# Four weight sums of an S5 layer moved from GpSimd to accumulating transfers, and one unit's state products put ahead of its Toeplitz products

## The chip, the cores and the metric

The kernel runs on one core of one Trainium2 chip, as one launch. The metric is the device time of a whole execution in microseconds; the median of several runs is compared. Times inside an execution are those of one profiled execution, counted from its first instruction.

The engines are named as in the profile: PE is TensorE's matmul and PEld its weight load, DVE is VectorE, ACT ScalarE, POOL GpSimd, SP SyncE, which only issues transfers. A queue with a q behind its name (ACTq, SPq) is an engine's issuing of transfers.

## The reference

One layer of a diffusion backbone over 1024 latent tokens of width 1024 and a prefix of 256 context tokens: a bidirectional S5 mixer (a diagonal complex state-space model in 64 groups of 16 channels with 64 states each), then a SwiGLU network, each behind an RMS norm with shift, scale and gate.

```python
lam_bar = jnp.exp(lam * jnp.exp(log_step)[:, None])
b_bar = ((lam_bar - 1.0) / lam)[..., None] * lax.complex(b_re, b_im)
bu = jnp.einsum('lgh,gnh->lgn', u, b_bar)
h = associative_scan(...)                      # h[l] = lam_bar * h[l-1] + bu[l]
y = jnp.einsum('lgn,ghn->lgh', h, c_mat).real  # forward and backward summed
...
y = y + d_skip * h
g = gelu(y);  y = g * sigmoid(g @ w_glu + b_glu)
x = x + gate * y
x = x + gate2 * ((silu(h2 @ w1) * (h2 @ w3)) @ w2)
```

## The kernel before

The sequence is cut into chunks of T = 8 tokens: 32 chunks of context, 128 of latent tokens. States are computed only at chunk ends. What a chunk adds within itself is a Toeplitz matrix per group; what the state at its start adds is a product with output weights. So the mixer's output for one group is a sum of two products: inputs of the chunk times a Toeplitz matrix (line 936), and states times output weights (line 926).

The 64 groups form four quarters q (16 groups each) and eight units k (8 groups each, two units to a quarter). Two lists of short words, `PROG1` and `PROG2`, are read from left to right by `run`, and give the order in which instructions are issued on every engine; each engine takes its own in that order. The scan itself is issued ahead of `PROG1` and is one chain on VectorE, with small fills between its steps; `PROG1` runs beside it on the other engines. The words that matter here:

- `Cqp`: the output weights CL of quarter q, part p (p = 0 to 3: real or imaginary, forward or backward). GpSimd forms two products of 128 x 1024 elements, one into CL, one into a buffer `ct` (line 78, as every `tensor_tensor`); then the two are added. How they are added is said by a letter of `HOWS`, one group of four letters for each quarter: `P` by two matmuls with the identity and a copy (673, 674), `E` by a sum on GpSimd (678, and 78 in the profile), `Y` by a transfer that adds while it writes, issued by GpSimd (676). The buffers `ct` are few: part 2 of quarter 2 and parts 1 and 3 of quarter 3 use the one in `rw`, parts 0 and 2 of quarter 3 share one in `ra`. A product that writes such a buffer waits until the transfer that reads it is done.
- `K2q`, `K2q+1` (so K4, K5 for quarter 2, K6, K7 for quarter 3): from CL, the short kernel matrices of the quarter (lines 813 to 821), copied by ScalarE (825) and written to memory `kd` (826). They need all four parts of CL.
- `Tu`: the load of a Toeplitz matrix from `kd`, issued by SP (834). Unit k uses T2k and T2k+1. There are four buffers.
- `Rk`: a copy on ScalarE of the unit's backward states in reversed order, first half (906). `Zk` is the same for the second half, in `PROG2`.
- `Pk`: the unit's Toeplitz products (16 matmuls, into two banks) and then the state products of the first half (64 matmuls) on top. `pk`: the state products alone, for the last two units, whose Toeplitz products come later. `Xk` and `Sk` are the two halves of `Pk` apart.
- `Y2k`, `Y2k+1`: copies of the two banks by ScalarE (988).
- `Nk`, in `PROG2`: the second half's state products, for the last two units with their Toeplitz products; `w`, `l`: loads of the gate weights on SP, behind the last `T`.

The order around the change: `... C21 C22 C23 R2 X2 K4 K5 S2 Y4 Y5 R3 P3 Y6 Y7 T8 T9 T10 T11 C30 C31 R4 P4 Y8 Y9 C32 C33 f7 M2 m0 R5 P5 Y10 Y11 R6 p6 Y12 Y13 R7 K6 p7 Y14 Y15 K7 T12 T13 T14 T15`. `f7` is a fill of states of the last unit on GpSimd. Banks for the units' products come from a ring of three, so a unit's second bank waits for a copy of the unit before.

Of the kernel before, what the change touches and what calls it, by code (L numbers as in the profile page):

```python
# [23 lines left out]
T = 8  # L24
G = 64
HC = 16
NS = 64
EPS = 1e-6
MAGIC = 12582912.0
HOWS = "PPPP PPEE PEEE EEEE"  # L30
ZEN = "VVSVSVSV"
PROG1 = ("A22 B0 A26 C02 G1 A30 A34 C03 A40 K0 A44 A48 C10 K1 L2 A54 G2 C11 A60 F10 C12 F11 C13 T0 T1 T2 T3 A64 M0 M1 K2 K3 R0 P0 Y0 Y1 L3 R1 C20 P1 Y2 Y3 T4 "
         "T5 G3 T6 T7 C21 C22 C23 R2 X2 K4 K5 S2 Y4 Y5 R3 P3 Y6 Y7 T8 T9 T10 T11 C30 C31 R4 P4 Y8 Y9 C32 C33 f7 M2 m0 R5 P5 Y10 Y11 R6 p6 Y12 Y13 R7 K6 p7 Y14 Y15 K7 T12 T13 T14 T15")
PROG2 = ("Z0 N0 Z1 Z2 D0 Z3 N1 D1 Z4 H0 H1 N2 D2 H2 N3 Z5 D3 H3 N4 D4 Z6 Z7 I0 J0 I1 J1 w0 w1 l1 H4 N5 D5 I2 J2 H5 I3 J3 W0 W1 x0 x1 x2 x3"
         " N6 D6 H6 I4 J4 N7 D7 b0 I5 J5 H7 g03 g13 I6 J6 g23 g05 g15 I7 J7 V1 w20 w21 g26 x10 x11 x12 x13")
LOG2E = 1.4426950408889634
# [7 lines left out]
def s5_ffn_kernel(tc, a, out):  # L44
    nc = tc.nc
    V, S, E, PE, SY = nc.vector, nc.scalar, nc.gpsimd, nc.tensor, nc.sync
    ctx = ExitStack()
    with ctx:
# [5 lines left out]
        def view(reg, kb, shape, parts=P):  # L54
            off = int(round(kb * 256))
            n = int(np.prod(shape))
            v = reg[:parts, off:off + n]
            if len(shape) > 1:
                names = "abcdef"[:len(shape)]
                v = v.rearrange(f"p ({' '.join(names)}) -> p {' '.join(names)}",  # L60
                                **{k: d for k, d in zip(names, shape)})
            return v
# [60 lines left out]
        U = view(RU, 0, [G, 160])  # L123
# [7 lines left out]
        def pool(name):  # L131
            p_ = tc.tile_pool(name=name, bufs=1, space=bass.MemoryType.PSUM, reuse_waits="tile")
            return p_, p_.__enter__()
# [11 lines left out]
        def pw(shape=(4, P)):  # L145
            return pW.tile([P] + list(shape), F32, tag="w", name="pw", bufs=NW[0])
# [627 lines left out]
        def zeros(t):  # L774
            S.copy(t, cpk[:, 0:1].to_broadcast([P, 15 * HC]))
            return t
# [133 lines left out]
        def flat(t):  # L910
            return t.rearrange("p t h -> p (t h)")
# [1 line left out]
        def yview(k, gp):  # L913
            return Y[:, k].rearrange("p t (a e h) -> p e a t h", e=2, h=HC)[:, gp]

        def states_mm(k, pts, half, hs, start):

            for a_ in range(4):
                for ri in range(2):
                    for d in range(2):  # L920
                        cs_ = slice(64 * (half ^ d), 64 * (half ^ d) + 64)
                        c0 = 31 + 64 * half
                        for gp in range(2):
                            ps = slice(64 * gp, 64 * gp + 64)
                            st = hs[ps, :, ri, a_] if d else STQ[k // 2][ps, c0:c0 + 64, ri, 8 * (k % 2) + a_]
                            PE.matmul(flat(pts[gp][cs_, a_]), st, flat(CL[k // 2][ps, ri, d, 4 * (k % 2) + a_]),
                                      start=start and ri == 0, stop=ri == 1 and (start or a_ == 3))

        def x_mm(k, pool):

            pts = [pool([4, T, HC]) for _ in range(2)]
            for a_ in range(4):
                for gp in range(2):
                    g = 2 * a_ + gp
                    kq = KQ[(2 * k + g // 4) % 4][:, g % 4].rearrange("p (t h) -> p t h", t=T)[:, ::-1]
                    PE.matmul(pts[gp][:, a_], U[:, 8 * k + g, 32:160], kq, start=a_ == 0, stop=False)
            return pts

        scan()
        inner = {}  # L940
        HSe = [view(r, kb, [64, 2, 4]) for r, kb in ((RC[3], 14), (RC[3], 12), (RC[3], 14), (RC[3], 12), (RA, 2), (RA, 0), (RA, 4), (RA, 6))]
        HSl = [view(RA, (4, 6, 0)[i] if i < 3 else STB * (i // 3) + 4.125 + 2 * (i % 3), [64, 2, 4]) for i in range(8)]
        Y7 = [view(RA, 8 + 2 * i, [4, T, HC]) for i in range(2)]

        def run(prog):


            for w in prog.split():
                op, i = w[0], int(w[1:])
                if op == "A":  # L950
                    ada(i)
                elif op == "M":
                    mod_cols(i)
                elif op == "K":
                    k_mats(*divmod(i, 2), [kt, zeros(pw([15 * HC])) if i < 4 else pm[:, 0:15 * HC]])
                elif op == "L":
                    cs_load(i, S)
                elif op == "G":
                    cs_sign(i)
                elif op == "B":  # L960
                    bb_put(1, bb_turn(1))
                    bb_put(0, bb_turn(0))
                elif op == "C":
                    q, part = divmod(i, 10)
                    for f in cl_ops(q, part, cts[q][part], HOW[q][part]):
                        f()
                elif op == "F":
                    fill(*divmod(i, 10), RC[3], 12)
                elif op == "f":
                    fill(i // 2, 1, RW, 0, (8 * (i % 2),))  # L970
                elif op == "T":
                    toeplitz(i)
                elif op == "R":
                    turned(i, 0, HSe[i], S)
                elif op == "Z":
                    turned(i, 1, HSl[i], ENG[ZEN[i]])
                elif op == "P":
                    inner[i] = x_mm(i, pw)
                    states_mm(i, inner[i], 0, HSe[i], False)
                elif op == "X":  # L980
                    inner[i] = x_mm(i, pw)
                elif op == "S":
                    states_mm(i, inner[i], 0, HSe[i], False)
                elif op == "p":
                    inner[i] = [pw([4, T, HC]) for _ in range(2)]
                    states_mm(i, inner[i], 0, HSe[i], True)
                elif op == "Y":
                    S.copy(Y7[i % 2] if i > 13 else yview(i // 2, i % 2), inner[i // 2][i % 2])
                elif op == "N":
                    late[i] = x_mm(i, pe8) if i > 5 else [pe8([4, T, HC]) for _ in range(2)]  # L990
                    states_mm(i, late[i], 1, HSl[i], i < 6)
                elif op == "D":
                    for gp, po in enumerate(late[i]):
                        tt(yview(i, gp), po, Y7[gp] if i == 7 else yview(i, gp), ADD)
                elif op == "H":
                    S.activation(Y[:, i], Y[:, i], AF.Gelu_apprx_tanh)
                elif op == "I":
                    if GH[0] is None:
                        GH[0] = tuple(view(region(t, 16, R32), 0, [4, 8, P]) for t in ("c1", "c0"))
                    late[i] = gt_hi(i, 0)  # L1000
                elif op == "J":
                    gt_lo(i, 0, late[i])
                elif op == "W":
                    if not WR:
                        W0.append(region("c2", 16, R32))
                        WR.append((view(W0[0], 0, [8 * 256]), view(W0[0], 8, [8 * 256])))
                    v = slice(1024 * i, 1024 * i + 1024)
                    split(wr0[i], (WR[0][0][:, v], WR[0][1][:, v]), E, V)
                elif op == "w":
                    cq, h = divmod(i, 10)  # L1010
                    SY.dma_start(wr0[h], a["w_glu"][cq][:, 1024 * h:1024 * h + 1024])
                elif op == "b":
                    SY.dma_start(bglu, a["b_glu"].to_broadcast([P, D]))
                elif op == "l":
                    load_glu(i)
                elif op == "m":
                    mod_row(0)
                elif op == "x":
                    gate(i % 10, slice(4 * (i // 10), 4 * (i // 10) + 4))
                elif op == "V":  # L1020
                    GR.append(region("ra", 80.5, R32))
                    GH[1] = (view(GR[0], 0, [4, 8, P]), view(GR[0], 16, [4, 8, P]))
                    WR.extend((view(GR[0], kb, [8 * 256]), view(GR[0], kb + 8, [8 * 256])) for kb in (32, 48, 64))
                    split(wraw, WR[i], E)
                elif op == "g":
                    glu_mm(0, i // 10, range(i % 10 + 1))
# [62 lines left out]

        HOW = [[{"P": PE, "Y": SY, "E": E, "V": V}[c] for c in h] for h in HOWS.split()]  # L1090
        run(PROG1)
# [99 lines left out]
        for cq in range(4):  # L1191
            for s in range(4):
                k = 4 * cq + s
# [300 lines left out]
        for f in list(PAIRS) + [NFT - 2]:  # L1494
            U = [("U", f, j) for j in range(7)]
# [5 lines left out]
            if f in PAIRS:  # L1501
                U = [("U", f + 1, j) for j in range(7)]
# [173 lines left out]
        for i, (kind, ft, j) in enumerate(seq):  # L1676
# [12 lines left out]
            if kind == "U":  # L1689
# [4 lines left out]
                if (ft, j) in LAST:  # L1694
                    k, h = LAST[ft, j]
# [63 lines left out]
```

## Time and profile before

| | |
|---|---|
| median of 3 runs | 1015.07 us (1015.01 to 1017.59) |
| the profiled execution, its own time | 1015.25 us |
| its span, first to last instruction | 1013.0 us |
| mean granted TensorE clock | 0.992 |
| busy: PE, DVE, POOL, ACT | 959.5, 781.8, 752.3, 441.7 us |
| `PROG1` beside the scan | from about 130 to 230 us |
| gate and SwiGLU matmuls | from about 259 us to the end |

How to read the rows. A row of the timeline has start, duration, engine, line, operation, written tile and read tiles, shape and count; merged rows give the first start and the time to the last end. What stands in brackets is the idle time before it and what ended it. A row of waits reads: who waited, for whom, total us, times, longest. A row of slices has the window, its length, busy time and instruction counts of each engine, the granted clock, the share of the transfer engines in use, and GB/s. Tiles have short names: `c` holds the four quarters' CL and buffers, `ra` the states and Toeplitz matrices, `ru` inputs and outputs, `pw`, `pe`, `kt` and `pm` are banks of PSUM.

### The profile page before, as it was taken

The page shows a single profiled execution, that of the slowest core. Times are in us where ns is not written, and L with a number is a line of the kernel's source. Part 1 is how long each engine was busy: PE and PEld are TensorE (multiplying, and loading weights), DVE is VectorE, ACT ScalarE, POOL GpSimd, SP SyncE. Part 2 cuts the span into 40 slices and gives each one's busy share as a digit, 9 for nine tenths or more (in the row PEclk, how much of TensorE's full clock was granted, in tenths as well). Part 3 has the DMA queues.
Part 4 walks back from the last instruction along what each step waited for, and adds up shares of the span by engine and source line. Part 5 has one row for each costly group of instructions (what it writes and reads, how often), then busy time and mean ns, then how long its engine had stood idle before and what let it go on. Part 6 is the DMA issues. An engine that isn't in the chain of part 4 may idle for free. (4 is left out here: it accounts for less than half of the span.)

```text
span 1013.0 us, 18603 instructions
## 1 busy us (share of the span) xinstructions
PE 959.5 (95%) x6988; PEld 770.5 (76%) x6988; DVE 781.8 (77%) x1694; ACT 441.7 (44%) x862; POOL 752.3 (74%) x574
## 2 busy tenths in 40 slices
PE   5988797878999999999999999999999999999996
PEld 1466423777999988778888888888888888888885
DVE  7979799995456867877958677686958677686987
ACT  5478622335544663443343343324343343424337
POOL 5799898980872448979785878777786877777674
PEclk9999999999999999999999999999999999999998
DMA  9765996324512021011212111121212111121205
GB/s 335 280 137 97 315 332 235 93 72 142 188 47 80 1 104 63 27 44 46 73 42 83 42 52 42 49 66 52 74 42 83 43 49 46 43 72 53 73 21 166
DMA packets 48545, 98.95 MB, mean 98 GB/s; under 512 B 4284, under 2 KB 18876, under 8 KB 47176
## 3 DMA queue, kind: packets, MB, share of 16 engines
q1 hardware_dynamic: 43272, 86.64, 25.9%
q0 software_dynamic: 2016, 7.34, 3.8%
q10 hardware_dynamic: 3168, 3.79, 1.1%
q8 instruction: 55, 0.90, 0.4%
q14 instruction: 34, 0.28, 0.1%
HBM read 84.25 MB, written 6.17 MB: 89 GB/s over the span
## 5 line engine op out<-in xcount | busy, mean ns | idle before, releaser
L78 POOL TENSOR_TENSOR c<-rxc,c 128x512 fp32r<-128x512 f32 x128 | 166.6, 1316 | 53.2 <-ACT c L1213 52.4
L1273 PE MATMUL ut<-ra,c 128*128 128x512 f32 x400 | 155.7, 389 | 1.2 <-DVE ra L78 1.2
L1272 PE MATMUL ut<-ra,c 128*128 128x512 f32 x400 | 155.7, 389 | 0.2 <-ACT ra L1213 0.2
L1274 PE MATMUL ut<-ra,c 128*128 128x512 f32 x400 | 155.6, 389 | 0.0
L1213 ACT CAST c<-rxc 128x512 fp32r<-128x512 f32 x128 | 79.0, 622 | 146.5 <-PE xt L1567 53.0
L1567 PE MATMUL xt<-c,c 128*128 128x512 f32 x540 | 129.7, 389 | 0.0
L78 DVE TENSOR_TENSOR ru<-ru,xt 128x1024 f32<-128x1024 f32 x90 | 107.8, 1216 | 13.4 <-PE xt L1567 9.4
L1567 PEld LDWEIGHTS xt<-c,c 128*128 128x128 f32 x540 | 101.4, 188 | 21.0
L78 DVE TENSOR_TENSOR ru<-ut,ru 128x512 f32<-128x512 f32 x98 | 67.2, 686 | 43.0 <-PE ut L1274 37.6
L1273 PEld LDWEIGHTS ut<-ra,c 128*128 128x128 f32 x400 | 75.1, 188 | 17.1 <-POOL rxc L78 1.5
L1272 PEld LDWEIGHTS ut<-ra,c 128*128 128x128 f32 x400 | 75.1, 188 | 16.1 <-ACT ra L1213 0.6
L1274 PEld LDWEIGHTS ut<-ra,c 128*128 128x128 f32 x400 | 75.1, 188 | 15.5
L78 POOL TENSOR_TENSOR c<-rw,c 128x512 fp32r<-128x512 f32 (+1 forms) x29 | 39.8, 1372 | 37.7 <-ACT c L1213 37.7
L78 POOL TENSOR_TENSOR c<-ru,c 128x512 fp32r<-128x512 f32 (+1 forms) x39 | 58.8, 1508 | 10.1 <-ACT c L1213 5.7
L1272 PE MATMUL ut<-c,c 128*128 128x512 f32 x160 | 62.3, 390 | 0.8 <-DVE rxa L78 0.8
L78 POOL TENSOR_TENSOR rxc<-rxc 128x512 f32<-128x512 f32 x40 | 61.5, 1537 | 1.6
L1273 PE MATMUL ut<-c,c 128*128 128x512 f32 x160 | 62.3, 389 | 0.0
L1274 PE MATMUL ut<-c,c 128*128 128x512 f32 x160 | 62.2, 389 | 0.0
L1567 PE MATMUL ut<-c,c 128*128 128x512 f32 x216 | 51.9, 389 | 0.0
L78 DVE TENSOR_TENSOR pe<-pe,ru 128x256 f32<-128x256 f32 x64 | 27.4, 428 | 29.3 <-ACT pe L1113 16.2
L585 PE MATMUL pv<-ru,c 128*64 128x160 f32 x512 | 44.4, 313 | 5.7 <-ACT rxa L389 1.8
L78 DVE TENSOR_TENSOR ru<-ru,ut 128x512 f32<-128x512 f32 x76 | 47.2, 679 | 0.3
(439 smaller groups left out, 2569.5 us busy)
## 6 DMA issues: line engine op xcount, KB each, us to landing
c<-in_ada_w SPq DMA_DIRECT2D x46, 256.0 KB
rxc<-in_w SPq DMA_DIRECT2D x38, 256.0 KB
rxc<-in_w SPq DMA_DIRECT2D x19, 512.0 KB
ru<-in_w SPq DMA_DIRECT2D x11, 512.0 KB
rw<-in_w SPq DMA_DIRECT2D x11, 512.0 KB
ra<-in_ada_w SPq DMA_DIRECT2D x10, 512.0 KB
ra<-in_ada_w SPq DMA_DIRECT2D x18, 256.0 KB
ru<-in_xT SPq DMA_DIRECT2D x4, 1024.0 KB
```

Of the source, the lines that this page charges most:

```text
L78: eng.tensor_tensor(out=o, in0=x, in1=y, op=op)
L585: PE.matmul(pv[64 * (i % 2):64 * (i % 2) + 64, ri, c0:c0 + 160], w[:, i, 64 * ri:64 * ri + 64], U[:, 8 * b + 4 * j + i], start=True, stop= ...
L1213: S.copy(o[0], x)
L1272: PE.matmul(pu, wh, bh, start=start, stop=False)
L1273: PE.matmul(pu, wh, bl, start=False, stop=False)
L1274: PE.matmul(pu, wl, bh, start=False, stop=stop)
L1567: PE.matmul(pd, w[:, cs_], b, start=j in (1, 2, 4) and n == 0, stop=n == 2, skip_group_check=j not in (1, 2, 4))
```

## The change

Two edits. In `HOWS` four letters go from `E` to `Y`: C22, C30, C31 and C32 are added by accumulating transfers of 512 KB, issued by GpSimd, instead of by sums on GpSimd. C23 and C33 stay as they are. In `PROG1` the word `P4` becomes `Q4`: the fifth unit's 64 state products of the first half are issued first, and its 16 Toeplitz products on top of them. For this `states_mm` and `x_mm` get arguments that say which of them opens and which closes the sum in a bank. The number of matmuls is the same.

```diff
-HOWS = "PPPP PPEE PEEE EEEE"
+HOWS = "PPPP PPEE PEYE YYYE"
...
-         ... C30 C31 R4 P4 Y8 Y9 C32 C33 f7 ...
+         ... C30 C31 R4 Q4 Y8 Y9 C32 C33 f7 ...
...
-        def states_mm(k, pts, half, hs, start):
+        def states_mm(k, pts, half, hs, start, alone=True):
...
-                                      start=start and ri == 0, stop=ri == 1 and (start or a_ == 3))
-
-        def x_mm(k, pool):
-
-            pts = [pool([4, T, HC]) for _ in range(2)]
+                                      start=start and ri == 0 and (alone or a_ == 0),
+                                      stop=alone and ri == 1 and (start or a_ == 3))
+
+        def x_mm(k, pool, pts=None):
+            first = pts is None
+            if first:
+                pts = [pool([4, T, HC]) for _ in range(2)]
...
-                    PE.matmul(pts[gp][:, a_], U[:, 8 * k + g, 32:160], kq, start=a_ == 0, stop=False)
+                    PE.matmul(pts[gp][:, a_], U[:, 8 * k + g, 32:160], kq, start=first and a_ == 0, stop=not first and a_ == 3)
...
+                elif op == "Q":
+                    inner[i] = [pw([4, T, HC]) for _ in range(2)]
+                    states_mm(i, inner[i], 0, HSe[i], True, False)
+                    x_mm(i, pw, inner[i])
```

More of the change, by code (lines that the diff above doesn't have):

```diff
@@ L29 @@
 MAGIC = 12582912.0
-HOWS = "PPPP PPEE PEEE EEEE"
+HOWS = "PPPP PPEE PEYE YYYE"
 ZEN = "VVSVSVSV"
 PROG1 = ("A22 B0 A26 C02 G1 A30 A34 C03 A40 K0 A44 A48 C10 K1 L2 A54 G2 C11 A60 F10 C12 F11 C13 T0 T1 T2 T3 A64 M0 M1 K2 K3 R0 P0 Y0 Y1 L3 R1 C20 P1 Y2 Y3 T4 "
-         "T5 G3 T6 T7 C21 C22 C23 R2 X2 K4 K5 S2 Y4 Y5 R3 P3 Y6 Y7 T8 T9 T10 T11 C30 C31 R4 P4 Y8 Y9 C32 C33 f7 M2 m0 R5 P5 Y10 Y11 R6 p6 Y12 Y13 R7 K6 p7 Y14 Y15 K7 T12 T13 T14 T15")
+         "T5 G3 T6 T7 C21 C22 C23 R2 X2 K4 K5 S2 Y4 Y5 R3 P3 Y6 Y7 T8 T9 T10 T11 C30 C31 R4 Q4 Y8 Y9 C32 C33 f7 M2 m0 R5 P5 Y10 Y11 R6 p6 Y12 Y13 R7 K6 p7 Y14 Y15 K7 T12 T13 T14 T15")
 PROG2 = ("Z0 N0 Z1 Z2 D0 Z3 N1 D1 Z4 H0 H1 N2 D2 H2 N3 Z5 D3 H3 N4 D4 Z6 Z7 I0 J0 I1 J1 w0 w1 l1 H4 N5 D5 I2 J2 H5 I3 J3 W0 W1 x0 x1 x2 x3"
```

## The prediction

> **What bounds the kernel now.** I read the page first, then the stage of the change in slices of ten, then the engines' rows in that stage.
>
> ```profile
> span 1013.0 us, 18603 instructions
> PE 959.5 (95%) x6988; PEld 770.5 (76%) x6988; DVE 781.8 (77%) x1694; ACT 441.7 (44%) x862; POOL 752.3 (74%) x574
> ```
>
> TensorE is busy 95% of the span, so the question is what the other 5% wait for, and whether the edited stage is among it.
>
> ```profile
> core 0: us, PE busy (x) PEld busy (x) DVE busy (x) ACT busy (x) POOL busy (x), PEclk, DMA share, GB/s
> 200.00:210.00 10.00, 7.42 (x148) 6.63 (x144) 10.00 (x58) 3.64 (x8) 9.92 (x6) 1.00 0.40 93
> 210.00:220.00 10.00, 8.46 (x160) 7.55 (x161) 9.74 (x56) 3.18 (x6) 9.84 (x5) 1.00 0.24 65
> ...
> 250.00:260.00 10.00, 10.00 (x178) 9.52 (x177) 6.20 (x11) 3.96 (x6) 6.90 (x4) 1.00 0.37 112
> ```
>
> From 200 to 220 TensorE has holes while VectorE (10.00, 9.74: the scan) and POOL (9.92, 9.84: the output weights) are full. From 250 TensorE is full. So the place where a microsecond can be had is before 250, and there are two candidates for the bound, the scan and POOL. Only POOL is relieved by the edit. Which of them ends last shows where they meet, at the eighth unit's turned copy, R7:
>
> ```profile
> 223.95 0.20 DVE L78 TENSOR_TENSOR ra<-ra,lta 128x64 f32<-128x64 f32 x1
> 224.24 0.62 ACT L906 COPY ra<-ra 128x512 f32<-128x512 f32 x1 [0.54 <-DVE ra L78]
> 225.27 0.19 PE L821 MATMUL kt<-rxc,rxa 64*16 64x16 f32 x1 [1.23 <-issue]
> 225.48 2.27 PE L926 MATMUL pw<-c,ra 64*64 64x128 f32 x64
> 225.64 0.36 ACT L825 COPY r<-kt 128x240 f32<-128x240 f32 x1 [0.78 <-PE pm L821]
> 230.48 1.22 PE L926 MATMUL pe<-c,ra 64*64 64x128 f32 x28 [0.47 <-ACT rw L825]
> ```
>
> R7 (the copy at 224.24) waits for the scan's last fill, which ends at 224.15; it is done at 224.86. The products that read it (p7, 225.48) follow the kernel matrices K6 on TensorE, whose last part comes after a stop of 1.23 us put down to issue. So p7 today is late by 225.48 - 224.86 = 0.62 us against the scan: that is all the room the scan leaves. The first products of the second half (N0, 230.48) wait for the copies of K7, which follows p7; so does all that comes after.
>
> **POOL's four sums.** The rows of before:
>
> ```profile
> 183.89 2.02 POOL L78 TENSOR_TENSOR rw<-rxc,rxa 128x1024 f32<-128x1024 f32 x1
> 185.99 2.36 POOL L78 TENSOR_TENSOR c<-c,rw 128x1024 f32<-128x1024 f32 x1
> 188.30 4.03 POOL L78 TENSOR_TENSOR c<-rxc,rxa 128x1024 f32<-128x1024 f32 x2
> 192.41 2.35 POOL L78 TENSOR_TENSOR c<-c,c 128x1024 f32<-128x1024 f32 x1
> 209.67 2.01 POOL L78 TENSOR_TENSOR ra<-rxc,rxa 128x1024 f32<-128x1024 f32 x1
> 218.18 2.36 POOL L78 TENSOR_TENSOR c<-c,rw 128x1024 f32<-128x1024 f32 x1
> ```
>
> and of the two accumulating transfers that the kernel already has on this line:
>
> ```profile
> 125.98 2.02 POOL L78 TENSOR_TENSOR rw<-rxc,rxa 128x1024 f32<-128x1024 f32 x1 [1.77 <-DMA c<-rw]
> 128.31 0.88 POOL L676 DMA_DIRECT2D c<-rw  x1 [0.30 <-POOL rw L78]
> 128.92 10.22 POOL L78 TENSOR_TENSOR c<-rxc,rxa 128x1024 f32<-128x1024 f32 x5
> ...
> DMA to landing us min/median/max: 6.1/7.5/8.8
> ```
>
> A sum on POOL takes, from the end of its product to the next product, 188.30 - 185.91 = 2.39 us; a transfer takes 128.92 - 128.00 = 0.92. Each exchange frees 1.47 us of POOL, four 5.9 us. It costs a landing: 6.1 to 8.8 us after the issue instead of 2.4.
>
> C22 (first of the four): its consumers are the kernel matrices K4, which today wait for the C23 sum that ends at 194.76 (1.5 us, in the rows of waits further down). With the transfer C23 ends 1.47 us earlier, at 193.3; C22 is issued at 186.2 and lands at 192.3 to 195.0. K4 wants it in its second half only. Gain at K4 between 0 and 1.47 us. I take 0.7, the middle, since the landing's median (193.7) is 0.4 behind C23's new end.
>
> C30, C31, C32: issued at about 197.5, 202.5 and 207.3 (C32's second product ends at 211.68 today, less three exchanges, 4.4). C32 multiplies into the buffer that C30's transfer reads, and C33 into that of C31's: five microseconds pass from an issue to that write, so POOL can stop there for 6.1 - 5 = 1.1 to 8.8 - 5 = 3.8 us, as it did 1.77 us at 125.98. Taken at the median landing: 2.5 us for C32's second product, and less for C33's, which is pushed back by it. The C33 sum, which ends at 220.54 now, then ends at 220.54 - 5.9 + 2.5 = 217.1 (214.7 without a stop, 218.5 with the longest), and C32's transfer lands at 207.3 + 2.5 + 7.5 = 217.3. Behind it POOL only has the fill of unit 7, which comes earlier by the same.
>
> **The fifth unit's order.** P4 today and what follows it:
>
> ```profile
> 207.59 0.63 ACT L906 COPY ra<-ra 128x512 f32<-128x512 f32 x1
> 208.15 1.13 PE L936 MATMUL pw<-ra,ru 128*128 128x128 f32 x8 [1.55 <-DMA ra<-kd]
> 210.12 1.16 PE L936 MATMUL pw<-ra,ru 128*128 128x128 f32 x8 [0.84 <-DMA ra<-kd]
> 213.41 0.49 PE L936 MATMUL pw<-ra,ru 128*128 128x128 f32 x2
> 219.16 0.63 ACT L906 COPY ra<-ra 128x512 f32<-128x512 f32 x1
> 219.93 2.67 PE L926 MATMUL pw<-c,ra 64*64 64x128 f32 x60 [0.61 <-ACT ra L906]
> ...
> PE kt L813 <- POOL c L78: 1.5, 1, 1.5
> ...
> PEld pw L926 <- POOL c L78: 0.3, 1, 0.3
> ```
>
> TensorE waits 1.55 + 0.84 = 2.39 us for the two Toeplitz transfers of this unit, and only then does the 64 state products, 2.1 us (211.28 to 213.41). The edit puts them into the hole, but not from its start: half of them read the turned copy R4, which ends at 208.22. So they run from 208.2 to 210.3, the second transfer has landed at 210.12, and the 16 Toeplitz products take 2.2 (1.13 + 1.16 less their overlap): the unit ends near 212.5 instead of 213.4. No matmul is added; the gain is 0.9 us, not 2.1, and it moves together with what C22 gives: 1.6 us by then (bounds 0.9 and 2.4). The other queues keep their order.
>
> P5 and its copies follow, 5.75 us from 213.41 to R6; its own two loads are issued right behind and were not waited for at 213.41, and may cost some tenths 1.6 us earlier. R6, 219.16 to 219.79 now, then ends at 218.2, and p6 takes 2.3 from there. It no longer meets the C33 sum, which held it for 0.33 us until 220.54; it wants C32, landing at 217.3 (bounds 213.4 and 218.5, the latter just behind R6). p6 ends at 220.5 instead of 222.6. K6 has 2.9 us with its stop (222.6 to 225.48): it ends at 223.4.
>
> **The sum.** K6 is then ahead of R7 by 1.5 us, and p7 goes by R7 alone: 224.86 and the 0.1 us to the matmul, 224.95 instead of 225.48. That is -0.5 us. The other 1.5 us of TensorE's gain, and POOL's 5.9, become idle time before the scan's end. VectorE's chain has no instruction added or removed. The copies of K6 stand behind R7 on ScalarE and move by 225.64 - 224.86 = 0.8; p7, K7, N0, the last Toeplitz loads and the gate weights behind them on SP's queue move by 0.5. From 250 on TensorE is full, so this passes to the end whole: span 1012.5. The profiled execution took 1015.25 us, 2.25 more than its span and 0.18 above the median of 1015.07. I forecast **1014.5** for the median. Its bounds are nothing gained (1015.1) and 0.6 plus the stop of 1.23 inside K6, if the waiting queue has fetched ahead by then (1013.2).
>
> **The rivals.**
>
> First, the engines are shared: the new transfers delay the Toeplitz loads, and the change ends slower.
>
> ```profile
> q0 software_dynamic: 2016, 7.34, 3.8%
> ```
>
> Fourteen accumulating transfers hold the 16 engines for 3.8% of 1013 us, 2.75 us each. C31's runs through just the loads of units 4 and 5. If they wait for all of it, the second load of unit 4 lands at 212.9; eight Toeplitz products are left then (1.1 us), so the unit ends at 214.0, 0.6 later than now. p6 gets back the 0.3 us of the C33 wait, and p7 starts 0.3 late: 1015.4. With C32's in the way too, 2.75 more: 1018.2. Against it: the share in use at 200 to 210 is 0.40, which leaves 6 us of free engine time. It decides from where that load lands some 2.4 us late (the unit's end then is the old one and those 0.3). 12%. The Trainium skill (DMA: Bandwidth & Descriptors, "Queues, rings and completion order") has each engine alternate between queues packet by packet, which speaks for this rival; no row of before shows the two queues together.
>
> Second, the hole before p7 lowers the clock.
>
> ```profile
> 241.00:242.00 1.00, 0.00 (x0) 0.00 (x0) 0.17 (x1) 0.79 (x1) 0.00 (x0) 1.00 1.11 247
> 242.00:243.00 1.00, 0.41 (x12) 0.41 (x16) 0.00 (x0) 0.77 (x2) 0.00 (x0) 1.00 1.05 247
> 243.00:244.00 1.00, 1.00 (x28) 1.00 (x26) 0.00 (x0) 0.00 (x0) 0.00 (x0) 0.60 1.04 335
> 244.00:245.00 1.00, 1.00 (x12) 0.67 (x7) 0.31 (x1) 0.00 (x0) 0.00 (x0) 0.50 1.01 414
> 245.00:246.00 1.00, 1.00 (x7) 1.00 (x6) 1.00 (x3) 0.26 (x1) 0.00 (x0) 0.50 1.07 442
> ```
>
> A hole of some 2 us at 241 is followed by three microseconds at a clock of 0.5 to 0.6, which costs about 0.4 + 0.5 + 0.5 and a little behind them, 1.6. The holes of 1.55 and 0.84 before P4 were followed by none. The new hole before p7 is 1.5 us beside the stop of 1.23 in K6. If it decides as the one at 241, 1014.5 + 1.6 = 1016.1; 13%. The other way round, the edit shifts the drop at 243 away: 1012.9; 8%. The Trainium skill (TensorE: Matmul & The Clock Gate, "What's actually happening") wants about 3.4 us idle for half the clock, so neither hole should do it, and by that rule 1014.5 stands; the trace differs, with 2 us, so I keep the chance.
>
> Third, the change doesn't act: C22 lands late and R4 comes late, so nothing reaches p7: 1015.1, 7%. Fourth, a gain over 3 us, for which the scan would have to end earlier: 3%; nothing in VectorE's row lets it.
>
> **How the numbers follow.** The forecast has 57%, with 1013.2 to 1015.4 for its own range; with the rivals above that makes 100. I take 1012.7 to 1016.8, which leaves out the far end of the first rival and the fourth; the three runs of before themselves lie 2.6 us apart. About 0.3% (3.0 us) is what can be told from no change: faster 0.04 (the fourth and a corner of the shifted clock), slower 0.06 (half of the first rival), same 0.90.
>
> **What would show it.** Right: four transfers on line 676 more, POOL without the four sums; 64 state products of the fifth unit ahead of its Toeplitz products, with a wait for a transfer between them under 1 us; R7 still released by VectorE at 224.2 and p7 within 0.2 us behind its end; N0 about 0.5 us earlier. Wrong: p7 still released by K6 or by a transfer, a wait of p6 for the landing of C32, a clock under 1.00 at 225 to 230, or a last fill of the scan that ends at another time than 224.15.

## The result and the profile after

| | before | after |
|---|---|---|
| median of 17 runs each, side by side | 1014.45 us (1012.01 to 1017.59) | 1019.07 us (1015.98 to 1022.67) |
| ratio, 95% interval | 1 | 1.0045 [1.0033, 1.0056] |
| the profiled execution, its own time | 1015.25 us | 1016.22 us |
| its span | 1013.0 us | 1014.4 us |

The change makes the kernel 4.6 us slower. The forecast was 1014.5, at most 1016.8. Behind the edit, lines 936, 988 and 1042 are 938, 994 and 1048.

The page of after: POOL has lost 5.5 us of work (752.3 before), TensorE's is the same:

```profile
span 1014.4 us, 18610 instructions
PE 959.3 (95%) x6988; PEld 771.6 (76%) x6988; DVE 781.8 (77%) x1694; ACT 441.4 (44%) x862; POOL 746.8 (74%) x574
```

POOL's timeline in after and, last, the landing of the transfers of line 676:

```profile
186.39 0.88 POOL L676 DMA_DIRECT2D c<-rw  x1 [0.30 <-POOL rw L78]
198.14 0.87 POOL L676 DMA_DIRECT2D c<-ra  x1 [0.30 <-POOL ra L78]
203.34 0.88 POOL L676 DMA_DIRECT2D c<-rw  x1 [0.30 <-POOL rw L78]
205.93 2.31 POOL L78 TENSOR_TENSOR ra<-rxc,rxa 128x1024 f32<-128x1024 f32 x1
208.54 0.88 POOL L676 DMA_DIRECT2D c<-ra  x1 [0.30 <-POOL ra L78]
213.56 2.36 POOL L78 TENSOR_TENSOR c<-c,rw 128x1024 f32<-128x1024 f32 x1
DMA to landing us min/median/max: 5.0/7.4/9.1
```

POOL did what the edit says: four issues in place of four sums, and its last sum ends at 215.92 instead of 220.54. What became of TensorE in after, with R4, the scan's last fill and R7 among its rows (a wait put down to issue is time in which the engine waited for nothing that the profile shows):

```profile
200.96 0.18 PE L821 MATMUL pm<-rxc,rxa 64*16 64x16 f32 x1 [2.02 <-issue]
210.27 0.63 ACT L906 COPY ra<-ra 128x512 f32<-128x512 f32 x1
210.95 2.26 PE L926 MATMUL pw<-c,ra 64*64 64x128 f32 x60 [0.52 <-ACT ra L906]
213.14 2.05 PE L938 MATMUL pw<-ra,ru 128*128 128x128 f32 x16
217.94 3.55 PE L938 MATMUL pw<-ra,ru 128*128 128x128 f32 x16 [2.75 <-DMA ra<-kd]
225.36 2.25 PE L926 MATMUL pw<-c,ra 64*64 64x128 f32 x60 [0.52 <-ACT ra L906]
224.11 0.21 DVE L78 TENSOR_TENSOR ra<-ra,lta 128x64 f32<-128x64 f32 x1
228.61 0.63 ACT L906 COPY ra<-ra 128x512 f32<-128x512 f32 x1
230.12 2.27 PE L926 MATMUL pw<-c,ra 64*64 64x128 f32 x64
235.40 1.22 PE L926 MATMUL pe<-c,ra 64*64 64x128 f32 x28 [0.47 <-ACT rw L825]
237.03 9.51 PE L926 MATMUL pe<-c,ra 64*64 64x128 f32 x292 [0.42 <-issue]
```

Q4 runs as meant (state products at 210.95, the Toeplitz products at 213.14 without a wait, done at 215.19). Then P5's Toeplitz products, which in before started at 213.41 without a wait, stand for 2.75 us for a load from `kd` and take 3.55 us instead of 2.05. The scan ends where it did (224.32 against 224.15), but R7 no longer waits for it: it comes 4.37 us later, in the wake of P5. p7 starts at 230.12 instead of 225.48, N0 at 235.40 instead of 230.48.

From P5 to p7 it adds up. Unit 4 ends 215.19 - 213.41 = 1.78 later (a stop of 2.02 for issue in K5, the row at 200.96, and a slow clock behind it delay R4 by 210.27 - 207.59 = 2.68; the new order gives 0.9 back, as forecast). Then 2.75 of waiting, and 1.00 from P5's first Toeplitz product to its last (3.55 in place of 2.55, with the 0.23 us wait of before in it): 5.53. Some 0.9 comes back (p6 2.25 without the wait for C33, against 2.67; K6 2.57 from 227.55 to p7, against 2.95): 4.64.

The same in two stages, before and then after; the clock is the column ahead of the last two:

```profile
200.00:232.00 32.00, 25.42 (x744) 22.61 (x740) 27.59 (x150) 11.45 (x24) 23.68 (x17) 1.00 0.27 72
232.00:248.00 16.00, 13.62 (x348) 12.77 (x352) 8.82 (x15) 8.73 (x11) 0.00 (x0) 0.89 0.69 206
```

```profile
200.00:232.00 32.00, 25.00 (x591) 23.10 (x592) 27.31 (x150) 9.40 (x19) 18.52 (x16) 0.89 0.47 109
232.00:248.00 16.00, 14.52 (x502) 13.56 (x498) 7.66 (x14) 9.55 (x14) 0.00 (x0) 1.00 0.50 144
```

From 200 to 232, after does 591 matmuls where before does 744. In the next stage before has a stop of 1.99 us from 240.6 on and a low clock behind it (0.89 over 16 us, some 1.8 us lost):

```profile
242.59 2.07 PE L926 MATMUL pe<-c,ra 64*64 64x128 f32 x36 [1.99 <-issue]
```

This execution of after has neither and gains 3.7 back: so this profile is only 1.4 us longer, and lies at the low end of its runs. Two more profiled executions of after have spans of 1020.1 and 1016.5, one more of before 1011.6; the means, 1017.0 and 1012.3, differ by 4.7 us, like the medians. From N0's first product to the end, the fourteen profiles of this case take 779.0 to 783.7 us: a delay of N0 passes on to the end, give or take such stops.

Why the loads are late. The loads of units 4 and 5 are four issues on SP, here merged (before, after), then the third load alone (before, after):

```profile
203.32 4.17 SPq L834 DMA_DIRECT2D ra<-kd  x4
204.66 0.90 SPq L834 DMA_DIRECT2D ra<-kd  x1
```

```profile
204.76 5.42 SPq L834 DMA_DIRECT2D ra<-kd  x4
206.99 1.43 SPq L834 DMA_DIRECT2D ra<-kd  x1
213.51 1.13 SPq L897 DMA_DIRECT2D rxa<-mbd  x1
```

P5 uses the third first. Before, it was there at most 213.41 - 204.66 = 8.8 us after its issue; after, 217.94 - 206.99 = 11.0. The transfer engines in slices of four, before and then after (the share in use is the last column but one):

```profile
204.00:208.00 4.00, 2.60 (x68) 2.28 (x66) 4.00 (x24) 1.37 (x3) 3.92 (x3) 1.00 0.48 104
208.00:212.00 4.00, 3.01 (x40) 2.73 (x44) 3.74 (x21) 0.22 (x1) 3.92 (x3) 1.00 0.60 140
```

```profile
204.00:208.00 4.00, 3.73 (x66) 3.30 (x62) 4.00 (x24) 1.59 (x3) 4.00 (x3) 0.99 0.79 132
208.00:212.00 4.00, 2.92 (x78) 2.53 (x76) 3.73 (x23) 1.59 (x3) 3.65 (x4) 1.00 0.88 185
```

And the queues from 200 to 222 in after (packets, MB, share of that window): the accumulating transfers hold the engines for 36.3% of 22 us, 8.0 us, in packets of 3.6 KB; the queue of the loads, `m0` among them, for 5.7 us in packets of some 0.7 KB on the mean.

```profile
q0 software_dynamic: 405, 1.46, 36.3%
q1 hardware_dynamic: 2224, 1.57, 25.9%
```

The clock of after behind the wait, in slices of one:

```profile
218.00:219.00 1.00, 1.00 (x5) 1.00 (x6) 1.00 (x7) 0.00 (x0) 0.92 (x4) 0.50 0.55 210
219.00:220.00 1.00, 1.00 (x7) 1.00 (x7) 1.00 (x7) 0.00 (x0) 0.40 (x3) 0.50 0.22 78
220.00:221.00 1.00, 1.00 (x6) 1.00 (x6) 1.00 (x7) 0.00 (x0) 0.00 (x0) 0.50 0.01 4
```

Behind the wait for the load TensorE runs at half its clock for some three microseconds; that is the 3.55 in P5's row. A wait of 1.9 us or more for a load comes with such a fall in all three profiles of after, and below in the transfers alone and the late pair; in the other nine profiles, whose waits for a load are 1.55 us at most, the clock doesn't fall between 212 and 230.

### The profile page after: what moved, and what is told of

Read it like the earlier page. It is cut to its first block, busy times and chain, and to the rows that moved or that the text cites. A ratio compares the mean times of both kernels' runs of the same rounds, so it can differ in the third digit from the quotient of the medians.

```text
span 1014.4 us, 18610 instructions
## 1 busy us (share of the span) xinstructions
PE 959.3 (95%) x6988; PEld 771.6 (76%) x6988; DVE 781.8 (77%) x1694; ACT 441.4 (44%) x862; POOL 746.8 (74%) x574
## 5 line engine op out<-in xcount | busy, mean ns | idle before, releaser
L78 POOL TENSOR_TENSOR c<-rxc,rxa 128x1024 f32<-128x1024 f32 x23 | 47.8, 2171 | 0.1
```

Of the source, the lines that this page charges most:

```text
L78: eng.tensor_tensor(out=o, in0=x, in1=y, op=op)
```

## The experiments

The theory (S): the new transfers share the engines with the Toeplitz loads of units 4 and 5, which come late. The rivals: O, the new order is at fault; M, the load `m0` on SP, issued at 213.51 instead of 218.13 because `M2`, ahead of it, no longer waits; T, each transfer costs the same wherever it stands; L, what costs is the late landing of the sums, not the loads; C, stops of TensorE that belong to the one execution profiled. Each edit below is made to after, if nothing else is said. Medians of before stand beside each group run together. A lag is p7's start less the start of the scan's last fill: 225.48 - 223.95 = 1.53 us in before, 230.12 - 224.11 = 6.01 in after.

**Each edit alone** (before: 1016.01).

```diff
 # transfers alone
-... R4 Q4 Y8 Y9 ...
+... R4 P4 Y8 Y9 ...
 # order alone
-HOWS = "PPPP PPEE PEYE YYYE"
+HOWS = "PPPP PPEE PEEE EEEE"
```

> The four transfers alone, with the old order P4. Theory S (the new transfers share the engines, so the Toeplitz loads of units 4 and 5 and TensorE's own instructions arrive late): as slow as both edits or slower, +4 to +6 us on before, with TensorE waiting 2 us or more for a load ahead of P5 or P4 and p7 at 229 or later (225.5 before, 230.1 with both edits). Rival O (the new order is at fault): within 1 us of before, p7 at 225 to 226. Rival M (the mod-row load m0, which POOL's earlier end lets SP issue at 213.5 instead of 218.1, crowds the loads): like theory S here.

> The new order Q4 alone, all four sums on GpSimd. Theory S: no slower than before, -0.5 us (+-1), the state products in the hole ahead of the Toeplitz products, no wait of more than 1 us for a load at P5, p7 at 225 to 225.5. Rival O: +3 to +5 us, with the wait of 2.75 us ahead of P5.

The transfers alone: 1022.34 us, 1.0054 [1.0034, 1.0075]. The order alone: 1013.79, 0.9985 [0.9974, 0.9997]. The rows of the transfers alone:

```profile
214.03 2.04 PE L938 MATMUL pw<-ra,ru 128*128 128x128 f32 x8 [4.26 <-DMA ra<-kd]
218.12 2.08 PE L938 MATMUL pw<-ra,ru 128*128 128x128 f32 x8 [2.06 <-DMA ra<-kd]
234.63 2.27 PE L926 MATMUL pw<-c,ra 64*64 64x128 f32 x64
```

and of the order alone:

```profile
213.64 2.27 PE L938 MATMUL pw<-ra,ru 128*128 128x128 f32 x18
216.15 1.83 PE L938 MATMUL pw<-ra,ru 128*128 128x128 f32 x14 [0.23 <-ACT ru L994]
226.35 2.27 PE L926 MATMUL pw<-c,ra 64*64 64x128 f32 x64
```

Without the new order, P4 stands at the same loads for 4.26 + 2.06 = 6.3 us, against 2.39 in before. Here the loads are issued late too: the first at 208.10, 5.1 us after K5's last write to `kd`, for which it waits (issued at 202.96); with the order alone these are 205.27 and 2.6 us. C31's transfer, issued at 203.13, runs beside that write; that it is what delays it is argued from these times. With the order alone, unit 4's and P5's Toeplitz products run through. O falls; all of the loss is in the transfers. The order is worth 0.15% without them, with an interval that nearly reaches 1.

**The transfers made small** (same group). Each new transfer adds an eighth of the rows, 64 KB; the rest of these four sums is left out.

```diff
-                    E.dma_start(o, ct, accum_op=ADD)
+                    w_ = slice(0, 8 if q == 0 else 1)
+                    E.dma_start(o[:, w_], ct[:, w_], accum_op=ADD)
```

> Both edits, but each of the four new transfers adds only the first eighth of its weights (64 KB for 512 KB; the other seven eighths are left out of the sum). GpSimd's instructions, their order and its early end stay; the bytes go. Theory S: the loss is gone, -0.5 us (+-1) on before, no wait for a load over 1 us at P5, and p7 at 224.9 to 225.3, held by the scan. Rival M: still +3 to +5 us, since m0 is issued as early as with both edits. Rival O: still +3 to +5.

1013.85 us, 0.9985 [0.9974, 0.9996]: the same as the order alone. Its R7 and p7:

```profile
224.53 0.62 ACT L907 COPY ra<-ra 128x512 f32<-128x512 f32 x1 [0.31 <-DVE ra L78]
225.77 2.27 PE L927 MATMUL pw<-c,ra 64*64 64x128 f32 x64
```

POOL issues all four transfers here and skips the four sums, and `m0` is early too (213.64); only seven eighths of the bytes are gone. So the loss is in the bytes, and POOL's earlier end (its last sum ends at 216.06 instead of 220.54), with R7 held by the scan again, is worth nothing beside the order alone.

**`m0` behind the last load** (same group).

```diff
-... C32 C33 f7 M2 m0 R5 P5 ... T12 T13 T14 T15
+... C32 C33 f7 M2 R5 P5 ... T12 T13 T14 T15 m0
```

> Both edits, with the mod-row load m0 issued behind the last Toeplitz loads instead of ahead of them. Theory S with the transfers alone: as slow as both edits, +4 to +5 us, P5's wait stays at 2 us or more. Rival M: the wait ahead of P5 falls under 1 us and 2 to 4 us of the loss go.

1019.0 us, 1.0033 [1.0015, 1.005]. The loss stays, so M falls as its cause, as it does by the small transfers. Theory S expected a wait of 2 us or more at P5, and this profile doesn't show it: stops in K4 and K5 (2.02 and 3.03 us) delay the users of the loads too, and P5 waits 0.37 us only.

**Which transfers** (before: 1014.21). C22 and C30 alone, C31 and C32 alone, C31 alone, each with the new order:

```diff
-HOWS = "PPPP PPEE PEYE YYYE"
+HOWS = "PPPP PPEE PEYE YEEE"   # early pair
+HOWS = "PPPP PPEE PEEE EYYE"   # late pair
+HOWS = "PPPP PPEE PEEE EYEE"   # C31 alone
```

> Q4, with transfers for C22 and C30 only; C31 and C32 are summed on GpSimd again. Theory S in its sharper form (what counts is a transfer issued while the Toeplitz loads of units 4 and 5 run, from 203 to 214): no loss, between -2.5 and +0.5 us on before, as the new order alone, and no wait of more than 1 us for a load at P5. Rival T (each transfer costs the same, wherever it stands): +1.5 to +3 us, half of what both edits lose.

> Q4, with transfers for C31 and C32 only; C22 and C30 are summed on GpSimd. Theory S: nearly the whole loss of both edits, +3 to +5 us, with a wait of 2 us or more for a load at P4 or P5. Rival T: +1.5 to +3.

> Q4, with a transfer for C31 alone; the other three are summed on GpSimd. It is issued near 205 to 206, when the loads of units 4 and 5 are being issued. Theory S: one transfer of 2.75 us of all engines, so units 4 and 5 wait 1 to 3 us for a load, +1 to +3 us on the new order alone. Rival T: +0.5 to +1.5.

The early pair: 1014.06, 1.0003 [0.9984, 1.0022]. The late pair: 1021.58, 1.0076 [1.0053, 1.0099]. C31 alone: 1016.26, 1.0021 [1.0005, 1.0037]. The late pair's waits:

```profile
217.96 1.75 PE L938 MATMUL pw<-ra,ru 128*128 128x128 f32 x8 [1.95 <-DMA ra<-kd]
221.45 2.08 PE L938 MATMUL pw<-ra,ru 128*128 128x128 f32 x8 [1.74 <-DMA ra<-kd]
```

C31 alone: unit 4's second load is issued at 206.44 and ends its wait at 216.34; the last row is its one transfer in the queue from 200 to 222.

```profile
206.44 0.57 SPq L834 DMA_DIRECT2D ra<-kd  x1
216.34 1.16 PE L938 MATMUL pw<-ra,ru 128*128 128x128 f32 x8 [1.18 <-DMA ra<-kd]
q0 software_dynamic: 144, 0.52, 15.0%
```

The early pair, two transfers like the late one, has no wait at P5 and no loss against before: T falls. What counts is whether a transfer meets the loads. The late pair is slower than all four, which no run explains; without the two early exchanges its transfers are issued 2.7 us later (206.06 and 211.29), nearer to the use of the loads. Beside C31 alone that load takes 9.9 us; in before, issued at 203.99 and waited for until 210.12, it took 6.1 (5.9 in the second profile). So one transfer of 512 KB delays a load by 3.8 us, while holding the engines for 15.0% of 22 us, 3.3 us. The Trainium skill (DMA: Bandwidth & Descriptors, "Queues, rings and completion order") says that an engine goes round its queues packet by packet. By that rule, as an estimate, a load beside the transfer's nine packets on each engine is delayed by no more than the transfer's own engine time; the 3.8 measured lies 0.5 above the 3.3.

**The loads taken away** (before: 1015.0). Both edits, without T8 to T11; units 4 and 5 multiply by the matrices of units 2 and 3.

```diff
-                    toeplitz(i)
+                    if not 8 <= i < 12:
+                        toeplitz(i)
```

> Both edits, all four transfers at full size, but the four Toeplitz loads of units 4 and 5 (T8 to T11) are left out: these units multiply by the matrices of units 2 and 3, which lie in the same buffers. Theory S (the loss runs through these loads): no wait ahead of P5, p7 at 225 to 227, and the time is 0 to 3 us under before. Rival L (the loss is the late landing of the sums C31 and C32, for p6 or for GpSimd's next product): the loss stays, +3 us or more, with p6 or K6 waiting for a transfer.

1015.47 us, 0.9994 [0.997, 1.0018]. All four transfers are there, at full size and with their landings, but no load to delay: the loss is gone, and L with it. The profiled execution is the longest of its twelve, with stops of 3.00 and 2.68 us in K4 and K5, and its p7 starts at 229.83 instead of the 225 to 227 expected; but units 4 and 5 wait for no load in it.

**Foreign traffic** (with the which-transfers group). The order alone, and behind each of the four sums that after had replaced POOL issues a plain copy of 512 KB from memory to memory, which nobody waits for.

```diff
+                    if (q, part) in ((2, 2), (3, 0), (3, 1), (3, 2)):
+                        E.dma_start(dr.tile([P, D], F32, ...), a["w2"][P * part:P * part + P])
```

> The new order, all four sums on GpSimd, and behind each of the four sums that the change took away GpSimd issues a plain copy of 512 KB from one place in memory to another, which nothing waits for. Theory S: the loads at P4 or P5 come late by 1 us or more and the time rises by 2 to 5 us against the new order alone (which was -0.15% on before), though every weight is summed as before. Rival L (the loss is the landing time of the sums, which the products and the buffers wait for): as the new order alone, within 1 us (GpSimd's four issues of 0.6 us are off the path).

1015.78 us, 1.0021 [1.0002, 1.004]. Slower than before, but without the wait of 1 us or more for a load that theory S expected: its profile has none. The copies are a weaker rival for the engines (three hold them for 24.1% of 22 us, 1.8 us each), and this profile is the longest of its runs, with the scan's last fill starting at 226.08, later than in all others (223.88 to 225.06). What its rise over the order alone comes from stays open.

**Executions again.** The two kernels, profiled once more: after twice, before once.

> The changed kernel once more, for a second profile. Theory S: P5 waits for its load again, 2 us or more, and p7 starts 3 us or more behind the scan's last fill. Rival C (the wait of 2.75 us in the first profile was a matter of that execution, and the loss is TensorE's stops for issue and its clock): no wait over 1 us for a load.

> The changed kernel a third time, for the spread between its profiles: theory S and rival C expect the same as of the second.

> The kernel before once more, for a second profile. Theory S: the loads of unit 5 are not waited for, and p7 starts within 2 us behind the scan's last fill. Rival C: stops for issue of 1 to 3 us in K5, K6 and near 241, each now and then followed by a clock of 0.5, come and go between the two profiles of this kernel as they do between the others'.

After (1021.94 and 1018.35 us), one pair of rows each:

```profile
221.83 1.13 PE L938 MATMUL pw<-ra,ru 128*128 128x128 f32 x8 [2.13 <-DMA ra<-kd]
234.41 2.27 PE L926 MATMUL pw<-c,ra 64*64 64x128 f32 x64
```

```profile
218.25 3.78 PE L938 MATMUL pw<-ra,ru 128*128 128x128 f32 x16 [2.53 <-DMA ra<-kd]
230.29 2.27 PE L926 MATMUL pw<-c,ra 64*64 64x128 f32 x64
```

and before (1013.82 us):

```profile
214.86 1.83 PE L936 MATMUL pw<-ra,ru 128*128 128x128 f32 x14 [0.26 <-ACT ru L988]
225.93 2.27 PE L926 MATMUL pw<-c,ra 64*64 64x128 f32 x64
```

P5's wait stands in all three profiles of after (2.75, 2.13, 2.53 us) and in neither of before. C falls for it. Stops for issue move single executions by some microseconds all the same, as `m0` late and the no-loads run show.

All lags in one line, by ratio: order alone 2.1 us (0.9985), small transfers 1.5 (0.9985), before 1.5 and 1.2 (1), early pair 2.0 (1.0003), C31 alone 5.3 (1.0021), after 6.0, 5.9 and 9.4 (1.0045), transfers alone 10.7 (1.0054), late pair 8.5 (1.0076). Three don't follow: no loads 5.5 (0.9994), foreign 4.8 (1.0021), `m0` late 8.0 (1.0033). Each is the lag of one execution, with its stops in K4 and K5; in the first two that execution is the longest of its runs.

## Why the prediction was wrong

**What held.** The unit's order: 0.9 us, with no load wait behind Q4. The scan unmoved (its last fill ends at 224.32 instead of 224.15), R7 as the cap: in the small-transfer run R7 follows the scan and nothing more is to be had. From N0 on the delay passes to the end.

**Sizes that were off.** I let five microseconds pass between C30's issue and the product that rewrites its buffer, and so a stop of 2.5 us. It is 205.93 - 198.14 = 7.8; there was no stop, and the last sum ended at 215.92, not 217.1. An exchange freed less than the 1.47 us that I took: the next product starts 0.9 us after the end of the one before, but then takes 2.3 in place of 2.0 (at the last exchange 1.2 and 2.0), and POOL's last sum ends 4.6 us earlier, not 5.9; its busy time fell by 5.5. The 0.7 us at K4 did not come: its second half waits 0.4 us for C22's transfer and starts at 195.10, against 194.82 in before. By the forecast's own sum, in which R7 is the cap, none of this costs anything.

**The step that failed** is one clause, on P5: "its own two loads are issued right behind and were not waited for at 213.41, and may cost some tenths 1.6 us earlier". They cost 2.75, 2.13 and 2.53 us of waiting. I had priced the shared engines only as the first rival, for unit 4's second load, and set against it "the share in use at 200 to 210 is 0.40, which leaves 6 us of free engine time". That was the wrong window and the wrong measure. The loads fly from 204 to 212, where the rows of before show 0.48 and 0.60: 3.7 us are free there, and C31's and C32's transfers want 5.5 by my own 2.75 each. And free time on average does not keep a load out of the way: C31 alone, with the engines at 0.72 from 206 to 212, made one load 3.8 us late. The rival's far end, 1018.2, stood 3.1 above the median of before, the result 4.6. What it lacked is the clock: behind the wait TensorE is at half its rate for three microseconds, which in the profile is 1.5 us more in P5's Toeplitz products (3.55 against 2.05 for unit 4's). The wait (2.5 us on the mean) and the clock together are some 4 of the 6.1 us (0.60%) that lie between the order alone and both edits; where the rest goes is not shown.

**My second rival**, a hole that lowers the clock, was right in kind and in size, but at another place: I looked for it at p7, and it came at P5 and behind K5's stop (200.96). Both holes, of 2.75 and 2.02 us, are shorter than the 3.4 us that the Trainium skill (TensorE: Matmul & The Clock Gate, "What's actually happening") asks of an idle window. The rows differ from it.

**A move not counted**: `m0`, 4.6 us ahead on SP's queue. No run shows harm from it: it is as early with the small transfers, which lose nothing.

**Open.** K5's stop for issue is 1.6 to 3.0 us in the first profile of each of the ten changed programs, 1.9 and 0.8 in the two further ones of after (the last has 1.8 in K4 instead), but 0.3 and 0.6 in the two of before; also where nothing differs up to K5, as in the order alone. So it isn't the transfers, and it costs little (that kernel is the fastest here); what makes it was not found. Nor is it shown why the order alone gains 0.15%, more than its lag tells: the stop near 240.6, absent from that profile, comes and goes between executions of one program (1.99 and 0.88 us in before).

## What to carry to other kernels

Before work is handed to transfers, list which loads are in flight when they run and who waits for those: a transfer that nobody waits for can still make the kernel longer, through another queue's load. Take the share in use from the microseconds in which that load flies, and count the transfer's whole engine time on top of the load. Here the early pair cost nothing that could be measured, the late pair 0.76%, and the best kernel by its ratio is the order alone.

## What the hardware showed

- An accumulating transfer of 512 KB inside SBUF holds the 16 engines for 2.8 to 3.3 us and lands 5.0 to 9.1 us after its issue in after (4.6 to 9.5 over the other profiles with transfers of this size). Loads of 256 KB in small packets, waited for beside two or more of them, took 9.4 (second load, transfers alone) to 13.9 us (fourth load, late pair) from issue to use, against 6.1 for the second in before.
- The granted clock fell to 0.50 behind holes of 2.02 and 2.75 us in after and of 1.59 us in the transfers alone (K5), but not behind the 1.53 and 1.55 us in before. It stays there for about 3.4 us at a time: the time that was lost to it between 194 and 252 us is 1.7 us or a multiple in the five profiles of the two kernels (before 1.7 and 0; after 3.4, 5.1 and 5.1).
